# Moving the block placement of a triangular inverse from GpSimd to VectorE and ScalarE in a two-layer hybrid trunk

## The chip, the core and the metric

The kernel runs on one core of a Trainium2 chip. The metric is the device time of one execution in microseconds. The engines are named as in the profile: PE is TensorE, DVE VectorE, ACT ScalarE, POOL GpSimd, SP SyncE, which here issues DMAs. Each engine works through its own instructions strictly in order; semaphores tie the engines to each other.

## The reference

The kernel computes a trunk of two layers on 1024 frames of width 1024. Layer 0 mixes with two head groups side by side, eight RWKV-7 heads of 64 and four gated DeltaNet heads of 128. Layer 1 mixes with chunked attention of 16 heads. Each layer then has a squared-ReLU MLP of width 4096 and a gated per-layer embedding.

```python
for i in range(DEPTH):                                   # DEPTH = 2
    h = rmsnorm(x, norm_mix_g[i])
    if i % 2 == 0:
        y_a = rwkv7_group(...)                           # 8 heads x 64
        y_b = gdn_group(...)                             # 4 heads x 128
        mix = jnp.concatenate([y_a, y_b], -1) @ even_w_out[e]
    else:
        mix = chunk_band_attention(...) @ attn_w_out[o]
    x = x + mix
    hf = rmsnorm(x, norm_ffn_g[i])
    x = x + jnp.square(jax.nn.relu(hf @ mlp_w1[i])) @ mlp_w2[i]
    x = x + rmsnorm(p[i] @ ple_w_proj[i], ple_norm_g[i]) * jax.nn.sigmoid(x @ ple_w_gate[i])

# inside gdn_group, per chunk of 64 frames:
sol = lax.linalg.triangular_solve(amat, rhs, left_side=True, lower=True, unit_diagonal=True)
```

The triangular solve is what the change is about. The kernel solves it, for both head groups of layer 0, by inverting the unit triangular matrix of each chunk and head.

## The kernel before, in words

Layer 0's mixing takes the first 860 us or so; the MLP, the embedding and the whole of layer 1 follow. Layer 0's mixing is cut into 16 units, one behind the other: units 0 to 7 on the first 512 frames, 8 to 15 on the second, and in each half RWKV (a pair of heads) and DeltaNet (one head) in turn. Even units are RWKV and have eight 128 by 128 matrices to invert (two chunks of 64 side by side in each), odd units are DeltaNet and have four. A unit goes through the stages in, front, mid, back and post, each in a lane of its own. The lanes are Python generators that `Trunk.run` interleaves by estimated times; a scheduler then sets each engine's order by its own timeline of all instructions. Weights are split into a high and a low part (`whi` on ACT, L316, and `wlo` on DVE, L317), and products with them on TensorE (`dps`) fill the time between the lanes' small steps.

The inverse of a unit starts in its front. `inverse_start` (L405) writes the matrices N to DRAM (L409), reads their 16 by 16 diagonal blocks back as `subb` with one block to a partition (L413), and inverts all blocks at once on GpSimd by substitution (L421, L423, fourteen times L428 and L430, L431: result `sub`). It writes the result to DRAM as `z` (L433) and reads it as `Xp`, 128 partitions wide (L435). All these DMAs are on SP's queue.

`inverse_end` (L438), in the mid lane, then doubles the blocks: 16 to 32, 32 to 64, 64 to 128. Its steps, with `quad[i]` the partitions 32i to 32i+31:

- T16, Xp's transposes times a mask, on ACT (L455); TensorE's step 0 on them. GpSimd writes X2's left half, Xp times the mask (L461); ACT brings step 0 out as Z16 (L462).
- TensorE's step 1; DVE writes X2's right half (L468) and transposes X2, now the 32 by 32 inverses, into T2 (L469).
- TensorE's step 2 on T2; its results go to TZ, quad 1 by ACT and quad 3 by DVE (L480). GpSimd clears a corner of TZ (L481), copies T2's quads 0 and 1 into TZ (L483), and X2's four diagonal blocks into F, where the finished inverse is put together (L485).
- TensorE's step 3, copies to TZ (L492) and F (L494), and the last two steps with ACT's copies (L505).

TZ is taken anew from the pool `mid` for each inverse; Z16 and the two F tiles are permanent. TensorE's products of the inverse carry the name `iz`. Unit 14's neighbours in time are the weights and norms of the embedding (`xg`, `praw`, L1750 on). `PMQ` (L992) is an RWKV unit's masked product, which TensorE needs for `ch`; `S` is its state.

Of the kernel before, what the change touches and what calls it, by code (L numbers as in the profile page):

```python
# [8 lines left out]
F32 = mybir.dt.float32  # L9
# [3 lines left out]
ALU = mybir.AluOpType  # L13
# [4 lines left out]
P = 128  # L18
# [94 lines left out]
class Trunk:  # L113
# [324 lines left out]
    def inverse_end(self, Xp, B, N, F):  # L438

        nc, h2 = self.nc, self.mid  # L440
        V, A, G = nc.vector, nc.scalar, nc.gpsimd
        cur, curT = Xp[:, :, 0:16], Xp[:, :, 16:32]
        m1, m2 = self.half[:, 0:1], self.half[:, 1:2]
        quad = [slice(32 * i, 32 * i + 32) for i in range(4)]
# [5 lines left out]
        def new(nm, w):  # L450
            return h2.tile([P, N, w], F32, tag=nm, name=nm)
# [5 lines left out]
        for g in range(N):  # L457
            for q in quad:
                self.mm(pz[q, g, :], B[q, g, q], T1[q, g, :], start=True, stop=True)
        X2, T2 = new("X32", 32), new("T32", 32)  # L460
        G.tensor_scalar(X2[:, :, 0:16], cur, m1, None, op0=ALU.mult)  # L461
        A.activation(self.Z16[:, 0:N, 0:16], pz, AF.Copy, scale=m2)  # L462
# [5 lines left out]
        V.scalar_tensor_tensor(X2[:, :, 16:32], cur, m2, px, op0=ALU.mult, op1=ALU.add)  # L468
        V.transpose(T2.rearrange("p g c -> p (g c)"), X2.rearrange("p g c -> p (g c)"))  # L469
        yield f"inverse{N}_1"  # L470

        pz = bank(32)

        TZ = new("TZ", 64)
        Z = TZ[:, :, 0:32]
        for g in range(N):
            for i in (0, 2):
                self.mm(pz[quad[i + 1], g, :], B[quad[i], g, quad[i + 1]], T2[quad[i], g, :], start=True, stop=True)
        for i, cp in ((0, A.copy), (2, V.tensor_copy)):
            cp(Z[quad[i + 1]], pz[quad[i + 1]])  # L480
        G.memset(TZ[quad[0], :, 32:64], 0.0)  # L481
        for i in range(2):
            G.tensor_copy(TZ[quad[i], :, quad[i]], T2[quad[i]])  # L483
        for i in range(4):
            G.tensor_copy(F[quad[i], :, quad[i]], X2[quad[i]])  # L485
        yield f"inverse{N}_2"
# [29 lines left out]
    def layer0_in(self):  # L516
        nc, tc, a = self.nc, self.tc, self.a
        with ExitStack() as es:
# [3 lines left out]
            l0 = self.l0 = es.enter_context(self.pool("l0"))  # L522
# [24 lines left out]
            for t in self.F.values():  # L547
                for i in range(1, 4):
                    nc.gpsimd.memset(t[32 * i:32 * i + 32, :, 32 * (i // 2 * 2):32 * i] if i % 2 else t[64:128, :, 0:64], 0.0)

            self.bm = self.pre.tile([P, 2, 2, 2, C], F32, tag="ph", name="bm")
            for h in range(2):
# [306 lines left out]
    def rwkv_front(self, p, hf, sc, raws, u):  # L859
        nc, h2, fr, sm, psm = self.nc, self.h2, self.fr, self.sm, self.psm  # L860
        V, A, G = nc.vector, nc.scalar, nc.gpsimd
# [28 lines left out]
        L = fr.tile([P, 4, C + 1], F32, tag="LE", name="L", bufs=2)  # L890
        G.memset(L[:, :, 0:1], 0.0)
        for c in range(4):
# [1353 lines left out]
```

## Time and profile before

| what | value |
|---|---|
| median of 3 runs | 2970.08 us (2968.52 to 2975.79) |
| profiled execution | 2974.58 us |
| its span | 2972.9 us |
| mean granted TensorE clock | 0.986 |
| busy: PE, DVE, ACT, POOL | 97%, 71%, 49%, 15% of the span |
| PE busy from 100 to 860 us | 715.34 of 760 us |
| POOL busy from 100 to 860 us | 290.36 of 760 us |

A row of a group reads: line, engine, operation, output<-input, shapes, count | busy us, mean ns of one | idle time of the engine just before them, with what ended most of it. A row of the timeline reads: start, duration, engine, line, operation, count, and in brackets the idle time of the engine before it with what released it. A row of waits reads: who waited, for whom; us in total, times, longest.

### The profile page before, as it was taken

The numbers are of one execution on the slowest core, as the hardware profiler recorded it, in microseconds if no ns is written. First come the engines' busy times: TensorE is split into PE (matmuls) and PEld (weight loads), VectorE is DVE, ScalarE is ACT, GpSimd is POOL, SyncE is SP. The second block draws the span as 40 slices with busy tenths as digits, with TensorE's granted clock in tenths as the row PEclk, the third lists the DMA queues.
The fourth block names the chain that finished last, engine by engine and source line by source line (L and its number), as shares of the span: only waits on it lengthen the run. The fifth ranks groups of instructions, "written<-read, shape, count | busy, mean of one in ns | idle before, by whom it ended". The sixth has DMA issues, their size and how long they took to land.

```text
span 2972.9 us, 46975 instructions
## 1 busy us (share of the span) xinstructions
PE 2888.2 (97%) x17286; PEld 2418.2 (81%) x17286; DVE 2108.3 (71%) x4183; ACT 1463.3 (49%) x2892; POOL 442.4 (15%) x951
## 2 busy tenths in 40 slices
PE   8899999999999999999999999999999999999999
PEld 6677777777777888888888999999888888888887
DVE  7565664556749777787786677776868777877884
ACT  5353432334437555544444466665847455544441
POOL 5443432333500000000000111111300000000000
PEclk9998999999899999999999999999999999999999
DMA  6534323332447444754433211110376444754423
GB/s 222 193 126 149 110 67 133 121 107 92 138 153 237 159 149 142 263 171 151 156 110 128 80 49 44 59 56 21 118 244 202 149 149 156 268 169 151 147 95 117
DMA packets 205159, 412.52 MB, mean 139 GB/s; under 512 B 46352, under 2 KB 48640, under 8 KB 204928
## 3 DMA queue, kind: packets, MB, share of 16 engines
q1 hardware_dynamic: 174112, 353.40, 36.0%
q10 hardware_dynamic: 30816, 56.11, 4.9%
q8 instruction: 136, 2.23, 0.3%
q14 instruction: 95, 0.78, 0.1%
HBM read 283.54 MB, written 125.89 MB: 138 GB/s over the span
## 4 chain that ended last, share of the span: by engine, by line
PE 65%; DVE 6%; DMA 4%; ACT 2%; issue 1%; POOL 1%; SPq 0%; POOLq 0%; ACTq 0%; DVEq 0%
PE dps L180 58%; PE po L180 2%; PE pt L195 1%; DMA pn<-pnd 1%; PE sn L180 1%; PE ch L180 1%; DVE pb L2094 1%; PE sf L180 1%; DVE act L1326 0%; POOL sub L430 0%; PE iz L180 0%; DVE F L2036 0%; POOL subt L428 0%; PE dps L195 0%; DVE r L1326 0%
## 5 line engine op out<-in xcount | busy, mean ns | idle before, releaser
L180 PE MATMUL dps<-r,act 128*128 128x512 f32 x3720 | 873.7, 392 | 1.4 <-DVE r L1326 0.8
L180 PEld LDWEIGHTS dps<-r,act 128*128 128x128 f32 x3720 | 698.1, 188 | 156.2 <-DVE r L1326 1.2
L180 PE MATMUL dps<-xg,whi 128*128 128x512 f32 x1248 | 423.0, 419 | 17.3 <-ACT whi L316 12.0
L180 PE MATMUL dps<-wq,act 128*128 128x384 f32 x1536 | 302.8, 341 | 4.3 <-ACT act L365 1.8
L180 PEld LDWEIGHTS dps<-xg,whi 128*128 128x128 f32 x1248 | 230.6, 196 | 67.9 <-ACT whi L316 12.6
L180 PEld LDWEIGHTS dps<-wq,act 128*128 128x128 f32 x1536 | 263.8, 189 | 7.4 <-DVE vs L1977 2.3
L180 PE MATMUL dps<-xg,wlo 128*128 128x512 f32 x624 | 253.6, 407 | 1.2 <-DVE wlo L317 1.1
L1325 ACT CAST act<-act 128x512 fp32r<-128x512 f32 (+2 forms) x281 | 159.5, 600 | 150.0 <-PE dps L180 64.9
L1326 DVE TENSOR_TENSOR act<-act 128x512 fp32r<-128x512 f32 (+2 forms) x281 | 178.1, 662 | 5.6 <-ACT act L1325 5.6
L180 PE MATMUL dps<-act 128*128 128x512 f32 x720 | 174.7, 391 | 0.9 <-DVE late L1447 0.9
L1325 ACT CAST act<-late 128x512 fp32r<-128x512 f32 x210 | 123.7, 620 | 104.4 <-PE dps L180 81.8
L180 PE MATMUL dps<-late,act 128*128 128x512 f32 x672 | 166.5, 392 | 0.0
L1326 DVE TENSOR_TENSOR act<-late,act 128x512 fp32r<-128x512 f32 x210 | 139.3, 687 | 33.3 <-ACT act L1325 33.2
L180 PEld LDWEIGHTS dps<-act 128*128 128x128 f32 x720 | 135.1, 188 | 30.8 <-DVE late L1447 1.4
L180 PEld LDWEIGHTS dps<-late,act 128*128 128x128 f32 x672 | 126.0, 188 | 27.7
L180 PEld LDWEIGHTS dps<-xg,wlo 128*128 128x128 f32 x624 | 121.9, 195 | 30.3 <-DVE wlo L317 3.4
L180 PE MATMUL dps<-xw,act 128*128 128x512 f32 x576 | 145.7, 392 | 0.4 <-DVE act L1326 0.4
L1593 DVE TENSOR_TENSOR xw<-xw,dps 128x512 f32<-128x512 f32 x192 | 130.1, 682 | 15.9 <-PE dps L180 15.8
L180 PEld LDWEIGHTS dps<-xw,act 128*128 128x128 f32 x576 | 107.9, 188 | 25.0 <-DVE act L1326 0.9
L1847 POOL MEMSET far<- 128x256 f32 x1 | 0.3, 316 | 799.7 <-PE dps L180 799.7
L2100 ACT ACTIVATE pb<-pb,mx 128x640 f32<-128x640 f32 (+4 forms) x128 | 89.2, 697 | 52.5 <-DVE mx L2094 51.5
L1325 ACT CAST r<-act 128x512 fp32r<-128x512 f32 x126 | 76.2, 617 | 57.0 <-PE dps L180 33.2
(517 smaller groups left out, 5363.2 us busy)
## 6 DMA issues: line engine op xcount, KB each, us to landing
hb<-late ACTq DMA_DIRECT2D x196, 256.0 KB
act<-hb SPq DMA_DIRECT2D x158, 256.0 KB
late<-in_w SPq DMA_DIRECT2D x60, 512.0 KB
act<-in_w SPq DMA_DIRECT2D x112, 256.0 KB
braw<-hb SPq DMA_DIRECT2D x80, 256.0 KB
wd<-whi SPq DMA_DIRECT2D x28, 512.0 KB
wd<-wlo SPq DMA_DIRECT2D x28, 512.0 KB
whi<-wd SPq DMA_DIRECT2D x28, 512.0 KB
```

What stands on the lines that cost most here:

```text
L180: return self.begin(self.nc.tensor.matmul(out, lhsT, rhs, start=start, stop=stop, skip_group_check=again))
L195: return self.begin(self.nc.tensor.transpose(out, in_, ident))
L1325: A.copy(hi, s)
L1326: V.tensor_tensor(lo, s, hi.bitcast(F32), op=ALU.subtract)
L1593: V.tensor_tensor(x[n][:, hs[hf]], x[n][:, hs[hf]], ps, op=ALU.add)
L1847: nc.gpsimd.memset(self.far, 0.0)
L2094: V.tensor_tensor_reduce(pb[:, (j0 - f0) * P:(j0 - f0 + n) * P], ps[:, 0:n * P], t, op0=ALU.add, op1=ALU.min, scale=-1.0, scalar=mx[:, 0:1 ...
L2100: A.activation(S, S, AF.Exp, bias=mx[:, 1:2] if nf else mx[:, 0:1], scale=-1.0, accum_out=l)
```

## The change

The change rewrites who does the small moves in `inverse_end`:

- TZ becomes one permanent tile, whose corner is cleared once when layer 0 is set up. T2 is no tile of its own any more: it is TZ's left columns.
- DVE's one transpose of 128 partitions becomes two that write into TZ: partitions 0 to 95 into the left columns (also step 2's operand), and quad 1 into the columns 32 to 63. GpSimd's two copies (L483) and its memset (L481) go.
- X2's left half is written by DVE instead of GpSimd (L461 before, L462 after).
- F's four diagonal blocks are copied by DVE (quads 2 and 0) and ACT (3 and 1) instead of GpSimd (L485 before, L482 after).
- The first column of the scan tile L in the RWKV front is cleared by DVE instead of GpSimd (L891 before, L890 after).

Lines from L461 to L480 stand one further down in the new file or keep their number; those behind some way up to about L890 stand three to one further up (L492 becomes L489, L505 becomes L502, L992 becomes L991).

```diff
--- before.py
+++ after.py
@@ -438,7 +438,7 @@
     def inverse_end(self, Xp, B, N, F):
 
         nc, h2 = self.nc, self.mid
-        V, A, G = nc.vector, nc.scalar, nc.gpsimd
+        V, A = nc.vector, nc.scalar
         cur, curT = Xp[:, :, 0:16], Xp[:, :, 16:32]
         m1, m2 = self.half[:, 0:1], self.half[:, 1:2]
         quad = [slice(32 * i, 32 * i + 32) for i in range(4)]
@@ -457,8 +457,9 @@
         for g in range(N):
             for q in quad:
                 self.mm(pz[q, g, :], B[q, g, q], T1[q, g, :], start=True, stop=True)
-        X2, T2 = new("X32", 32), new("T32", 32)
-        G.tensor_scalar(X2[:, :, 0:16], cur, m1, None, op0=ALU.mult)
+        X2, TZ = new("X32", 32), self.TZ[:, 0:N]
+        T2, Z = TZ[0:96, :, 0:32], TZ[:, :, 0:32]
+        V.tensor_scalar(X2[:, :, 0:16], cur, m1, None, op0=ALU.mult)
         A.activation(self.Z16[:, 0:N, 0:16], pz, AF.Copy, scale=m2)
         yield f"inverse{N}_0"
         px = bank(16)
@@ -466,23 +467,19 @@
             for q in quad:
                 self.mm(px[q, g, :], self.Z16[q, g, :], cur[q, g, :], start=True, stop=True)
         V.scalar_tensor_tensor(X2[:, :, 16:32], cur, m2, px, op0=ALU.mult, op1=ALU.add)
-        V.transpose(T2.rearrange("p g c -> p (g c)"), X2.rearrange("p g c -> p (g c)"))
+        V.transpose(T2, X2[0:96])
+        V.transpose(TZ[quad[1], :, 32:64], X2[quad[1]])
         yield f"inverse{N}_1"
 
         pz = bank(32)
 
-        TZ = new("TZ", 64)
-        Z = TZ[:, :, 0:32]
         for g in range(N):
             for i in (0, 2):
                 self.mm(pz[quad[i + 1], g, :], B[quad[i], g, quad[i + 1]], T2[quad[i], g, :], start=True, stop=True)
         for i, cp in ((0, A.copy), (2, V.tensor_copy)):
             cp(Z[quad[i + 1]], pz[quad[i + 1]])
-        G.memset(TZ[quad[0], :, 32:64], 0.0)
-        for i in range(2):
-            G.tensor_copy(TZ[quad[i], :, quad[i]], T2[quad[i]])
-        for i in range(4):
-            G.tensor_copy(F[quad[i], :, quad[i]], X2[quad[i]])
+        for i, cp in ((2, V.tensor_copy), (3, A.copy), (0, V.tensor_copy), (1, A.copy)):
+            cp(F[quad[i], :, quad[i]], X2[quad[i]])
         yield f"inverse{N}_2"
         px = bank(32)
         for g in range(N):
@@ -548,6 +545,8 @@
                 for i in range(1, 4):
                     nc.gpsimd.memset(t[32 * i:32 * i + 32, :, 32 * (i // 2 * 2):32 * i] if i % 2 else t[64:128, :, 0:64], 0.0)
 
+            self.TZ = l0.tile([P, 8, 64], F32, tag="TZ", name="TZ")
+            nc.gpsimd.memset(self.TZ[0:32, :, 32:64], 0.0)
             self.bm = self.pre.tile([P, 2, 2, 2, C], F32, tag="ph", name="bm")
             for h in range(2):
                 nc.gpsimd.memset(self.bm[64 * (1 - h):64 * (2 - h), :, h], 0.0)
@@ -888,7 +887,7 @@
         A.activation(lw, psw, AF.Tanh, bias=self.dv["hw0"][:, p:p + 1], scale=0.5)
         V.tensor_scalar(lw, lw, -0.5 * EXPM05, -0.5 * EXPM05, op0=ALU.mult, op1=ALU.add)
         L = fr.tile([P, 4, C + 1], F32, tag="LE", name="L", bufs=2)
-        G.memset(L[:, :, 0:1], 0.0)
+        V.memset(L[:, :, 0:1], 0.0)
         for c in range(4):
             V.tensor_tensor_scan(L[:, c, 1:C + 1], self.ones, lw[:, c * C:(c + 1) * C], 0.0,
                                  op0=ALU.mult, op1=ALU.add)
```

TensorE issues the same number of instructions; DVE issues 72 more, ACT 32 more, POOL 135 fewer. The table of estimated times is the same in both kernels; the scheduler orders anew. From the end of layer 0's mixing on the order of every engine is the same as before. In the part that changes, SP gets the small transfers z, Xp and subb of some units ahead of weight loads that stood before them, and ACT in unit 0's inverse has T16 of the next unit and then the cast `bh` ahead of the TZ copy, where before it had `bh`, T16 and the TZ copy.

Unit 2 on DVE, before, from the product f of a later unit on to the second PMQ:

```order
L1122 SCALAR_TENSOR_TENSOR f<-f 128x512
L1146 TENSOR_TENSOR cs<-cs,gs_beta 128x4
L868 SCALAR_TENSOR_TENSOR f<-raw,vecs,f 128x512
L1050 SCALAR_TENSOR_TENSOR S_1987<-S_1923,ee,ch 128x64
L1147 TENSOR_SCALAR ncs<-cs 128x4
L992 TENSOR_TENSOR PMQ<-pm,mask_136 128x384
L1014 SCALAR_TENSOR_TENSOR Sh<-S_1987,ee,blkr 128x128
L1014 SCALAR_TENSOR_TENSOR Sh<-Sr_184,ee,blkr 128x128
L992 TENSOR_TENSOR PMQ<-pm,mask_136 128x384
```

And after, from the same f on:

```order
L1121 SCALAR_TENSOR_TENSOR f<-f 128x512
L1144 TENSOR_TENSOR cs<-nu 128x4
L1147 SCALAR_TENSOR_TENSOR hin<-ss,nu 128x4
L867 SCALAR_TENSOR_TENSOR f<-raw,vecs,f 128x512
L462 TENSOR_SCALAR X_2505<-Xp,half 128x8x16
L1145 TENSOR_TENSOR cs<-cs,gs_beta 128x4
L1049 SCALAR_TENSOR_TENSOR S_1985<-S_1921,ee,ch 128x64
L991 TENSOR_TENSOR PMQ<-pm,mask_136 128x384
L1146 TENSOR_SCALAR ncs<-cs 128x4
L1013 SCALAR_TENSOR_TENSOR Sh<-S_1985,ee,blkr 128x128
L1013 SCALAR_TENSOR_TENSOR Sh<-Sr_184,ee,blkr 128x128
L991 TENSOR_TENSOR PMQ<-pm,mask_136 128x384
```

X2 of unit 2 (`X_2505`) is new here, and S, PMQ and Sh, which stood behind the last f, now stand behind X2.

Unit 14 on DVE, before, in the norm of an earlier unit (vv, rv, rsw) and the split of an embedding weight (wlo):

```order
L707 TENSOR_TENSOR gate<-dps,acc 128x512
L1204 SCALAR_TENSOR_TENSOR W<-ch,gs_egc,b 128x128
L1073 TENSOR_SCALAR vv<-pp 128x8
L294 TENSOR_SCALAR rv<-vv 128x8
L297 TENSOR_TENSOR rsw<-rv 128x8
L298 SCALAR_TENSOR_TENSOR rsw<-rsw,vv 128x8
L299 SCALAR_TENSOR_TENSOR rv<-rsw,rv 128x8
L317 TENSOR_TENSOR wlo<-wraw,whi 128x1024
```

And after:

```order
L706 TENSOR_TENSOR gate<-dps,acc 128x512
L1203 SCALAR_TENSOR_TENSOR W<-ch,gs_egc,b 128x128
L1072 TENSOR_SCALAR vv<-pp 128x8
L294 TENSOR_SCALAR rv<-vv 128x8
L297 TENSOR_TENSOR rsw<-rv 128x8
L462 TENSOR_SCALAR X_9046<-Xp,half 128x8x16
L298 SCALAR_TENSOR_TENSOR rsw<-rsw,vv 128x8
L317 TENSOR_TENSOR wlo<-wraw,whi 128x1024
L299 SCALAR_TENSOR_TENSOR rv<-rsw,rv 128x8
```

X2 of unit 14 (`X_9046`) has come between L297 and L298, ahead of wlo.

Unit 4's substitution on POOL, before:

```order
L421 AFFINE_SELECT sub<-subb 64x16x16
L423 AFFINE_SELECT sub<-sub 64x16x16
L705 COPY raw<-h_g_192 128x3
L428 TENSOR_TENSOR subt<-sub,subb 64x14
L430 TENSOR_TENSOR sub<-sub,subt 64x14
L428 TENSOR_TENSOR subt<-sub,subb 64x2x13
L485 COPY F_230<-X_3087 32x4x32 x2
L430 TENSOR_TENSOR sub<-sub,subt 64x2x13
L485 COPY F_230<-X_3087 32x4x32 x2
L483 COPY TZ<-T_3088 32x4x32 x2
```

And after:

```order
L421 AFFINE_SELECT sub<-subb 64x16x16
L423 AFFINE_SELECT sub<-sub 64x16x16
L428 TENSOR_TENSOR subt<-sub,subb 64x14
L430 TENSOR_TENSOR sub<-sub,subt 64x14
L428 TENSOR_TENSOR subt<-sub,subb 64x2x13
L430 TENSOR_TENSOR sub<-sub,subt 64x2x13
```

The copies of unit 3 into F (`F_230`) and TZ have gone from between the first steps of the substitution, and a copy into `raw` has moved further back.

## The prediction

> **What bounds the kernel now.** I read the busy time in three windows first, to see which stage the change can reach; then the chain that ended last; then what TensorE waited for in the first 900 us; then the timeline round each of its inverse waits. The order of instructions on every engine is the same in both kernels from about 860 us on (the end of layer 0's mixing), so only the first two windows count. Columns: width, then busy time of PE, PE weight loads, DVE, ACT and POOL, the granted clock, DMA share, GB/s.
>
> ```profile
> 0.00:100.00 100.00, 89.61 (x404) 69.09 (x405) 69.52 (x129) 48.91 (x85) 54.69 (x133) 0.98 0.67 239
> 100.00:860.00 760.00, 715.34 (x6615) 572.46 (x6614) 456.60 (x1108) 298.43 (x730) 290.36 (x721) 0.95 0.36 119
> 860.00:2972.90 2112.90, 2083.20 (x10272) 1776.65 (x10270) 1582.22 (x2947) 1116.00 (x2078) 97.39 (x98) 1.00 0.42 141
> ...
> PE 65%; DVE 6%; DMA 4%; ACT 2%; issue 1%; POOL 1%; SPq 0%; POOLq 0%; ACTq 0%; DVEq 0%
> ```
>
> TensorE is the bound throughout. In the window of the 16 inverses (100 to 860 us) it is busy 715.34 of 760 us: 44.7 us of idle time, plus what the clock of 0.95 takes, is all that any rearrangement of small copies can win there. GpSimd, with 290.36 us, is far from full, and so are DVE and ACT. The next view gives how much of the idle time is the inverse's own (columns: total, times, longest).
>
> ```profile
> PE iz L180 <- DVE TZ L480: 10.2, 2, 9.3
> PE iz L180 <- ACT T L455: 6.6, 4, 2.5
> POOL sub L421 <- DMA subb<-scr: 83.8, 14, 23.1
> POOL X L461 <- DMA Xp<-z: 64.4, 14, 7.5
> ```
>
> TensorE lost 10.2 + 6.6 us in inverses. In 14 of 16 units the substitution begins by waiting for the DMA that brings its blocks (83.8 us), so GpSimd being free earlier does not start them sooner. And the X2 multiply, which the change hands to VectorE, waited 64.4 us for the DMA of Xp: on GpSimd that wait hurt nobody, on VectorE it may.
>
> **What leaves GpSimd.** These groups go (busy, mean ns, idle before):
>
> ```profile
> L485 POOL COPY F<-X 32x256 f32<-32x256 f32 x32 | 14.3, 447 | 23.7 <-DVE X L468 18.1 <-DVE rsw L302 4.3
> L485 POOL COPY F<-X 32x128 f32<-32x128 f32 x32 | 13.9, 434 | 28.2 <-DVE X L468 27.1
> L483 POOL COPY TZ<-T 32x128 f32<-32x128 f32 x16 | 7.3, 459 | 1.7 <-DVE T L469 0.8 <-DVE cc L914 0.2
> L483 POOL COPY TZ<-T 32x256 f32<-32x256 f32 x16 | 7.2, 451 | 0.7
> L461 POOL TENSOR_SCALAR X<-Xp,half 128x128 f32<-128x128 f32 x8 | 5.8, 729 | 37.3 <-DMA Xp<-z 37.3
> L461 POOL TENSOR_SCALAR X<-Xp,half 128x64 f32<-128x64 f32 x8 | 3.7, 465 | 32.2 <-DMA Xp<-z 27.1 <-PE iz L180 3.2 <-PE ch L180 2.0
> ```
>
> 14.3 + 13.9 + 7.3 + 7.2 + 5.8 + 3.7 = 52.2 us of busy time, and the small memsets. It is worth something only where a copy stood inside a later unit's substitution, because Xp then comes that much earlier.
>
> **What VectorE and ScalarE get.** Nearest rows of the same shapes:
>
> ```profile
> L469 DVE STREAM_TRANSPOSE T<-X 128x256 f32<-128x256 f32 x8 | 3.5, 438 | 0.2
> L469 DVE STREAM_TRANSPOSE T<-X 128x128 f32<-128x128 f32 x8 | 2.4, 300 | 0.1
> L480 DVE COPY TZ<-iz 32x256 f32<-32x256 f32 x8 | 3.4, 429 | 11.9 <-ACT TZ L480 11.7
> L468 DVE SCALAR_TENSOR_TENSOR X<-Xp,half,iz 128x128 f32<-128x128 f32 x8 | 2.7, 343 | 1.9 <-PE iz L180 0.9 <-issue 0.7 <-POOL sub L430 0.3
> L480 ACT COPY TZ<-iz x16: 257/310/364, 144.7 to 838.9; 32x256 f32<-32x256 f32 x8, 32x128 f32<-32x128 f32 x8
> ```
>
> VectorE per inverse: X2 at most 0.34 us, one transpose more (0.44 or 0.30), two F copies at most 0.43 each, so 1.64 us in a unit of eight matrices and 1.50 in one of four, 8 x 3.14 = 25 us at most in all. ScalarE: 2 x 0.31 x 16 = 10 us. Against 456.60 and 298.43 us busy in 760 us neither becomes the bound; what covers these is idle time of the two engines. The cover is thin where TensorE waits right behind the second transpose or an F copy; the F copies stand behind the TZ copies, which TensorE needs first. The bounds are 0 and 16 x 0.44 = 7 us (every added transpose on the path); I take +2, nearer to nothing since TensorE works on other lanes meanwhile and waits in few inverses at all.
>
> **Unit 4, where GpSimd's copies did hurt.**
>
> ```profile
> 261.81 1.54 POOL L485 COPY F<-X 32x128 f32<-32x128 f32 x2 [0.19 <-DVE X L468]
> 263.72 0.98 POOL L485 COPY F<-X 32x128 f32<-32x128 f32 x2
> 264.76 1.11 POOL L483 COPY TZ<-T 32x128 f32<-32x128 f32 x2
> ...
> 271.14 0.45 PE L180 MATMUL iz<-TZ,Ng 64*64 64x64 f32 x8 [1.51 <-POOL sub L430]
> ...
> 285.43 0.72 PE L180 MATMUL iz<-T,N 32*32 32x16 f32 x64 [1.71 <-ACT T L455]
> 286.98 1.65 PE L180 MATMUL pm<-AR,bm 128*128 128x128 f32 x4 [0.82 <-ACT tm L1004]
> ```
>
> Six copies of unit 3 (1.54 + 0.98 + 1.11 = 3.6 us) stand inside unit 4's substitution, and the stall at 271.14 is TensorE's wait for GpSimd at the same place. Without them T of unit 4 is there 3.6 us earlier, more than 1.71 + 0.82. All three stalls go: 1.51 + 1.71 + 0.82 = -4.0 us. Bounds: 0 (the transfers are late anyway) to -4.0; I take -4.0, since the rows name these releasers.
>
> **Unit 5.**
>
> ```profile
> 308.01 0.18 POOL L709 COPY h_r<-raw 128x1 f32<-128x1 f32 x1 [3.46 <-DVE raw L707]
> ...
> 327.50 0.35 ACT L455 ACTIVATE T<-Xp,half 128x64 f32<-128x64 f32 x1 [7.77 <-DMA Xp<-z]
> 328.88 1.05 PE L180 MATMUL pp<-ones,o 128*128 128x1 f32 x8 [2.03 <-ACT o L1222]
> ```
>
> This substitution was held 3.46 us by a halo copy; now that copy stands behind it. Xp then lands near 324 instead of 327.50, and the 2.03 us stall, an ACT result queued behind T, goes. X2 on VectorE now holds a cast, L707 and a weight split behind it, estimated at +0.8. Net -1.2; bounds -2.0 and +2.7 (Xp not earlier: the split about as late as X2 is).
>
> **Unit 1: the largest stall stays.**
>
> ```profile
> 145.69 0.26 PE L180 MATMUL iz<-X,TZ 32*32 32x32 f32 x2 [9.28 <-DVE TZ L480]
> ...
> 140.00:160.00 20.00, 14.31 (x128) 11.59 (x129) 4.89 (x8) 8.24 (x21) 4.17 (x13) 0.75 0.34 114
> ```
>
> DVE's TZ copy names itself here, but it was itself behind ScalarE's TZ copy, which is queued behind T of the next unit, which waits for Xp. In the new order T still stands ahead, with the bh cast now between: +0.8 (one 512-wide cast; between 0 and that). The granted clock of 0.75 in this stretch shows what a long stall costs besides itself. [...]
>
> **Unit 2: the new wait on VectorE.**
>
> ```profile
> 172.85 1.86 POOL L485 COPY F<-X 32x128 f32<-32x128 f32 x4
> 175.03 0.63 POOL L483 COPY TZ<-T 32x128 f32<-32x128 f32 x2
> ...
> 181.73 0.55 DVE L992 TENSOR_TENSOR PMQ<-pm,mask 128x384 f32<-128x384 f32 x1
> ...
> 183.15 0.55 PE L180 MATMUL ch<-b,PMQ 128*128 128x64 f32 x4
> 187.01 0.40 ACT L455 ACTIVATE T<-Xp,half 128x128 f32<-128x128 f32 x1 [3.50 <-DMA Xp<-z]
> ```
>
> In the new order X2 of unit 2 stands ahead of S and PMQ, which released TensorE's ch at 183.15. Xp comes 1.86 + 0.63 = 2.5 us earlier, near 184.5. Then X2 0.34, two small ones and PMQ 0.55 bring ch to about 185.6: +2.4 us. If Xp is not earlier, +4.9. I take +2.4, because both copy rows lie inside the substitution.
>
> **Unit 14: the same, and worse.**
>
> ```profile
> 740.88 0.17 DVE L297 TENSOR_TENSOR rsw<-rv 128x8 f32<-128x8 f32 x1
> 756.24 0.40 ACT L455 ACTIVATE T<-Xp,half 128x128 f32<-128x128 f32 x1 [4.65 <-DMA Xp<-z]
> 756.70 0.36 PE L180 MATMUL iz<-T,N 32*32 32x16 f32 x20 [2.47 <-ACT T L455]
> ```
>
> X2 now stands right behind the L297 of 740.88, with the rest of the norm and two weight splits behind it; in the old run Xp was used at 756.24, 15.4 us later. In the new order the blocks' DMAs go ahead of two activation loads and the front of this unit is issued some 6 us earlier (an estimate from the TensorE work that it is moved ahead of), and X2 leads Xp's arrival by less, but I expect VectorE to stand still for about 6 us of it and TensorE to lose 6.5 us in place of the 2.47: +4. Bounds 0 (the front comes early enough) and +11 (15.4 less the work that TensorE has queued, about 2, and the 2.47 that goes).
>
> The other units' X2 cost at most some tenths each, +0.5 in all; queue SP gets the inverse's small transfers earlier and weight loads a little later, which I cost at nothing, since the casts that use them come many us later; without that cover a late weight load would show as a TensorE wait for a whi or wlo.
>
> **Sum.** +2 (added transposes) - 4.0 (unit 4) - 1.2 (unit 5) + 0.8 (unit 1) + 2.4 (unit 2) + 4 (unit 14) + 0.5 = +4.5 us. The profiled execution took 2974.58 us (span 2972.9 and 1.7 around it), 4.5 above the median of 2970.08; 2974.58 + 4.5 = 2979.1 for a like execution, 2974.6 for the median. 0.3%, 8.9 us, is about what a measurement of this kernel can tell from no change, so the likeliest is no change, at 2974.
>
> **The rivals.** *Slower:* VectorE's in-order wait for Xp. It decides if Xp is not earlier than before: then unit 2 costs 4.9, unit 5 +2.7, unit 14 +11, with +2, +0.8 and +0.5 as above and no gain at unit 4: 22 us, 2992. For it speaks the 64.4 us that X2 waited on GpSimd; against it that the substitutions lose 2.5 to 3.6 us of copies in just the units where it matters. Chance 0.26. *Faster, by shorter substitutions:* unit 4's and 5's stalls go (4.0 + 2.0), the rest of T's waits too (6.6 - 1.71 = 4.9), and the 9.28 by a third as T's Xp comes earlier; X2 costs nothing: 6.0 + 4.9 + 3 = -14, 2956. The 83.8 us of waits for blocks speak against it. Chance 0.19. *Faster, by less contention:*
>
> ```profile
> L919 DVE TENSOR_TENSOR f<-f 128x512 f32<-128x512 f32 x7 | 6.5, 928 | 0.0
> L1326 DVE TENSOR_TENSOR act<-act 128x512 fp32r<-128x512 f32 (+2 forms) x281 | 178.1, 662 | 5.6 <-ACT act L1325 5.6
> ```
>
> The same elementwise operation takes 928 ns on VectorE while GpSimd works and 662 where it rests. With 52.2 of 345 us of GpSimd gone a sixth of this goes: (928 - 662) / 6 = 44 ns on each of about 500 (nearly half of the 1108 that VectorE runs in the window), 22 us of VectorE, of which half on the path would be -11: 2959. [...] Most of VectorE's time is off the path, so chance 0.07. *Nothing is felt:* all copies were hidden before and are now, 2970; it lies inside the likeliest case, which has 0.48 in all.
>
> **How the numbers follow.** Same 0.48; slower 0.26; faster 0.19 + 0.07 = 0.26. The range reaches from 2956 to 2990: beyond lie some 2 in 10, the far ends of the faster and the slower cases.
>
> **What would show it.** Right: no T copy of GpSimd and no stall at units 4's places; stalls of 2 to 6 us on TensorE released by PMQ near 184 and by a weight split or a norm near 745; the 9 us stall near 145 unchanged; DVE 25 us busier or less. Wrong: VectorE's X2 waits for Xp for under 2 us in all units (then the sum is near -6), or TensorE's idle time after X2 in units that I cost at tenths.

## The result: 2989.7 us, slower by 0.77%

The changed kernel takes 2989.70 us in the median of 6 runs (2986.82 to 2998.80), the kernel before beside it 2969.68 (2958.49 to 2975.79): a ratio of 1.0077, 95% interval 1.0053 to 1.0101. The forecast was no change, at 2974. The executions of one kernel lie up to 17 us apart before and 12 after; the profiled one of the changed kernel, 2998.17 us with a span of 2996.5, is one of its slowest. That 2989.70 lies just inside the end of the forecast range, 2990, is luck: the sum did not lead there. Two slow executions further down, 3624.87 us with the weight loads first (granted clock 0.747) and 6140.41 us with X2 alone (1.0), are left out of the times given there.

The same three windows, after (columns as in the prediction):

```profile
0.00:100.00 100.00, 87.79 (x382) 67.37 (x383) 66.59 (x125) 46.81 (x81) 47.95 (x119) 0.95 0.64 222
100.00:860.00 760.00, 705.46 (x6498) 565.01 (x6497) 462.47 (x1169) 307.74 (x753) 239.68 (x600) 0.94 0.35 118
860.00:2996.50 2136.50, 2102.39 (x10411) 1790.19 (x10408) 1593.75 (x2963) 1122.14 (x2091) 96.80 (x98) 1.00 0.42 141
```

In the second window GpSimd is 51 us less busy, but TensorE too does less: 705 for 715 us. In the first 880 us, before and after:

```profile
0.00:880.00 880.00, 823.08 (x7096) 655.84 (x7097) 535.88 (x1257) 354.73 (x826) 345.06 (x853) 0.95 0.40 134
```

```profile
0.00:880.00 880.00, 811.49 (x7010) 646.14 (x7011) 537.80 (x1308) 360.20 (x846) 287.63 (x718) 0.95 0.38 130
```

TensorE stands idle for 68.5 us where it stood for 56.9. The granted clock, summed up finer than the two digits of these rows, takes another 47.8 us where it took 40.7. So of the 24 us between these two executions about 12 are idle time and about 7 clock in this part.

The time that GpSimd got back became waiting. Who waited, in the first 900 us, after:

```profile
POOL sub L421 <- DMA subb<-scr: 146.6, 14, 22.9
ACT T L455 <- DMA Xp<-z: 74.3, 14, 14.7
DVE X L462 <- DMA Xp<-z: 42.3, 15, 7.5
PE iz L180 <- DVE TZ L480: 8.6, 4, 5.9
```

GpSimd waits 146.6 us for the blocks where it waited 83.8, and VectorE has a new wait of 42.3 us for Xp.

To see where TensorE lost time, its matmuls, which are the same in all the kernels, are counted as work at their usual spacing; what a stretch took beyond its work is lost in it. The sizes are estimates, since they depend on the spacing that is taken as usual; the differences between the columns move by 1 to 2 us with it. From one profiled execution each (us lost):

| stretch of TensorE's work (us) | before | changed | old work, new order | moved work, old order | new order, X2 late |
|---|---|---|---|---|---|
| 0 to 20 (to about 35 us) | 11.3 | 15.9 | 11.3 | 15.8 | 15.7 |
| 20 to 100 | 12.3 | 14.3 | 12.1 | 14.2 | 14.0 |
| 100 to 160 | 30.7 | 36.9 | 37.4 | 34.8 | 34.7 |
| 160 to 260 (units 3 to 5) | 41.2 | 37.8 | 42.1 | 30.8 | 36.1 |
| 260 to 340 | 33.3 | 37.7 | 43.4 | 36.8 | 36.3 |
| 340 to 520 | 43.1 | 44.5 | 40.6 | 47.1 | 40.4 |
| 520 to 700 (to the end of the mixing) | 51.5 | 57.0 | 56.6 | 49.4 | 60.3 |
| the rest of the kernel | 55.5 | 58.2 | 57.3 | 51.2 | 52.4 |

(The last three columns are experiments, below.) The changed kernel loses more at the start, round unit 2, in the stretch behind unit 5 (260 to 340) and in the one that holds unit 14, and 3.4 us less round units 3 to 5. The last row moves by 4 to 6 us between kernels with the same order there (51.2 and 55.5 in the old order, 52.4 to 58.2 in the new), so a single row of one execution is worth no more than that. The column of the moved work in the old order shows that kernel's fastest execution, 2975.86 us against a median of 2984.71: what the moved work costs is not in it.

Two corrections of what stands ahead: a DeltaNet or RWKV unit has four chunks of 128 frames (the eight matrices are four chunks of two heads), and the order differs at one more place, a few rows at the end of layer 1's attention, where the trace shows no loss that the other kernels with that order share.

### The profile page after: what moved, and what is told of

Same layout as the page of the kernel before. It is cut to its first block, busy times and chain, and to the rows that moved or that the text cites. A ratio compares the mean times of both kernels' runs of the same rounds, so it can differ in the third digit from the quotient of the medians.

```text
span 2996.5 us, 46894 instructions
## 1 busy us (share of the span) xinstructions
PE 2895.6 (97%) x17286; PEld 2422.6 (81%) x17286; DVE 2122.8 (71%) x4255; ACT 1476.7 (49%) x2924; POOL 384.4 (13%) x816
## 4 chain that ended last, share of the span: by engine, by line
PE 67%; DVE 13%; DMA 9%; ACT 3%; POOL 3%; issue 3%; SPq 0%; ACTq 0%; DVEq 0%; POOLq 0%
PE dps L180 56%; PE po L180 2%; DVE act L1325 2%; PE ch L180 2%; POOL subt L428 1%; PE pt L195 1%; POOL sub L430 1%; PE iz L180 1%; PE sn L180 1%; PE pm L180 1%; DMA late<-in_w 1%; DMA pn<-pnd 1%; DMA Xp<-z 1%; PE tp L180 1%; DMA wraw<-in_w_out 1%
## 5 line engine op out<-in xcount | busy, mean ns | idle before, releaser
L180 PE MATMUL po<-ptile,vs 128*128 128x256 f32 (+1 forms) x576 | 98.6, 282 | 5.3 <-ACT ptile L362 2.7
```

The lines of the kernel that those rows point to most:

```text
L180: return self.begin(self.nc.tensor.matmul(out, lhsT, rhs, start=start, stop=stop, skip_group_check=again))
```

## The experiments

**How an order is held.** In the kernels called "order tied" the list of an engine's instructions is taken from another kernel, one list for each engine, and each instruction is made to issue behind its forerunner, by an edge for order alone as the kernel itself sets them at L189 and L326. The tie added no time that a run shows: with the old order tied and X2 alone moved the ratio is 0.9996 (0.9985 to 1.0008). The lists themselves are left out here.

So work and order can be changed apart. Each ratio below is against the kernel before run beside the experiment, whose median lay between 2968.9 and 2972.0 us; compare ratios rather than times. Theory A was VectorE's wait for Xp (the prediction's slower rival), B the newly drawn order, C the added busy time.

### Work and order apart

Moved work, old order:

> The changed kernel's instructions, but every engine's order tied to that of the kernel before, so that the order is not drawn anew; X2's left half stands right ahead of the X2 multiply-add that follows it on VectorE (so it never waits for Xp there), the two transposes where the one was, the F copies right behind them, on ScalarE ahead of its TZ copy. Theory A (what costs is VectorE standing still for Xp in X2): about 2970, as before. Theory B (what costs is the order drawn anew, weight loads behind z among it): about 2970. Theory C (the added busy time of VectorE and ScalarE costs): 2980 or more. If GpSimd's relief gives something back, 2960 to 2966.

Measured: 2984.71 us, ratio 1.0045 (1.0030 to 1.0059). Of the three theories only C foresaw this.

Old work, new order:

> The kernel before's instructions, with the order of all instructions that both kernels have tied to that of the changed kernel, on every engine; the ones that only the kernel before has (GpSimd's copies, memsets and X2, VectorE's one transpose) are placed freely by the scheduler. VectorE never waits for Xp in X2, and GpSimd does the small moves. Theory A: 2970 to 2974. Theory B: 2985 to 2992. Theory C: about 2970.

Measured: 2992.06 us, 1.0075 (1.0060 to 1.0090). So this order costs the old work as much as the whole change costs, though in it VectorE never waits for Xp in X2; and the moved work costs 14 us in the old order, in which nothing was redrawn. Theories A and B alone fail on the first of these, theory C alone on the second. The two costs don't add up to more than 1.0077, and why is not shown. One rival for part of the second is untested: GpSimd's copies, memset and X2 are in no held list there, and where the scheduler put them some stand ahead of a later unit's substitution, which costs by itself (see the run up to unit 5 below).

The new order, with X2 alone moved in VectorE's list:

```diff
 # VectorE's list of the changed kernel, for each of the 16 units
-[..., X2 (L462), 6 to 56 rows of other work, X's other half (L469), ...]
+[..., 6 to 56 rows of other work, X2 (L462), X's other half (L469), ...]
```

> The changed kernel with its own order on every engine, in which one thing is moved: X2's left half on VectorE stands right ahead of the multiply-add that writes X2's other half, 6 to 56 rows later, where Xp has long landed. VectorE's 42 us of waits for Xp go. Theory A: 2972 to 2976, 14 to 18 us less than the changed kernel. Theory B: 2984 to 2990; only the stall at unit 2 (3.5 us and its half clock) goes, since the stall at unit 14 is released by a weight load. Theory C: 2988.

Measured: 2986.77 us, 1.0060 (1.0047 to 1.0074), against 1.0077 (1.0053 to 1.0101) for the changed kernel: 0.17% less by the ratios, 5 us (3 us by the medians), for 42 us of VectorE's waits, and the intervals overlap. Why so little can be seen at unit 2. TensorE's stall there in the changed kernel, then in this one, then with the old work in the new order:

```profile
193.03 1.11 PE L180 MATMUL ch<-b,PMQ 128*128 128x64 f32 x4 [3.47 <-DVE S L1049]
```

```profile
193.46 0.45 PE L180 MATMUL iz<-F,TZ 64*64 64x64 f32 x8 [2.25 <-ACT TZ L502]
```

```profile
189.05 0.48 PE L180 MATMUL iz<-F,TZ 64*64 64x64 f32 x4 [3.90 <-ACT TZ L505]
```

X2's wait is gone in the second and was never there in the third, and TensorE stands still all the same, for a step of an inverse. That this step now comes too early in TensorE's list is likely from these rows, but no run moved it alone.

Unit 14, with SP's list alone changed:

```diff
 # SP's list of the changed kernel at unit 14
-z<-sub, wraw<-in_w_ple, Xp<-z, wraw<-in_w_ple
+wraw<-in_w_ple, wraw<-in_w_ple, z<-sub, Xp<-z
```

> The changed kernel with its own order on every engine, in which one thing is moved: on SP's queue the two loads of the embedding's weight stand ahead of unit 14's z again, as they did before, and no longer behind its wait for GpSimd. Theory A: no change but tenths, 2989, since VectorE still waits 6.6 us for Xp there and the next weight split stands behind it. Theory B: the stall of 4.9 us for the weight goes, 2983 to 2985.

Measured: 2990.84 us (five executions), 1.0066 (1.0050 to 1.0082): no gain on the changed kernel's 1.0077 that the intervals would show. The changed kernel at that place, SP's queue, VectorE, ScalarE and TensorE:

```profile
757.02 0.45 SPq L433 DMA_DIRECT2D z<-sub  x1
757.57 0.53 SPq L310 DMA_DIRECT2D wraw<-in_w_ple  x1
...
764.21 0.28 DVE L462 TENSOR_SCALAR X<-Xp,half 128x128 f32<-128x128 f32 x1 [6.65 <-DMA Xp<-z]
...
761.64 1.04 ACT L316 CAST whi<-wraw 128x1024 fp32r<-128x1024 f32 x1 [7.36 <-DMA wraw<-in_w_ple]
...
762.74 2.07 PE L180 MATMUL dps<-xg,whi 128*128 128x512 f32 x4 [4.92 <-ACT whi L316]
```

VectorE waits 6.65 us for Xp, as forecast. But what holds TensorE for 4.92 us is a weight: its load stands behind z in SP's list, z waits for GpSimd's substitution to end (757.02), and the load is issued at 757.57. With the loads ahead of z:

```profile
762.51 1.19 PE L180 MATMUL dps<-xg,whi 128*128 128x512 f32 x4 [0.74 <-ACT whi L316]
766.75 0.71 PE L180 MATMUL iz<-T,N 32*32 32x16 f32 x34 [3.05 <-ACT T L455]
```

The stall is 0.74, and a new one of 3.05 us stands 4 us later, for the Xp that now comes second.

### One engine's order

TensorE's list alone tied to the old one, and TensorE's list alone tied to the new one:

> The changed kernel with only TensorE's order tied to that of the kernel before; the scheduler orders the other engines as it likes. Theory B, in the form that TensorE's newly drawn order does it (steps of the inverse with less other work between them): 2970 to 2976, most of the 20 us gone. Theory B in the form that the order of the other engines does it, or theory A (VectorE's waits for Xp): 2983 to 2990.

> The kernel before with only TensorE's order tied to that of the changed kernel; the scheduler orders the other engines as it likes. TensorE's order does it: 2985 to 2992. The other engines' orders do it: 2968 to 2975.

Measured: 2998.87 us, 1.0092 (1.0079 to 1.0105), and 2986.00 us, 1.0049 (1.0037 to 1.0061). The first lies outside all that was expected: the old list of TensorE did not bring the time back (1.0092 against 1.0077, intervals overlapping). The second is what was expected if TensorE's order does it. Neither run changes TensorE's list by itself, because the scheduler draws the other lists to fit: in the second, 91 of some 1250 VectorE operations in the first 900 us stand out of the order of "old work, new order", 202 out of the old one. In the first VectorE's list comes nearer to that of "moved work, old order" than to the changed kernel's (124 against 235 out of place), and yet the time is the worst of all, where exactly the old order gave 1.0045. So a list near the old one is not enough, and which engine's list costs most stays open.

The old work tied to the new order only up to unit 5 (330 us), and to the old one behind:

> The kernel before's instructions, tied to the changed kernel's order up to unit 5's inverse (about 330 us) and to the old order from there on. The profile of the kernel with the new order throughout had lost 7 to 9 us by that place of its 20: 2977 to 2980. If the new order does harm only as a whole: 2970 or 2990.

Measured: 2993.24 us, 1.0076 (1.0063 to 1.0088): as much as the new order throughout, where 7 to 9 us were expected. That does not show that the first third is enough. In its profile about 6 us are lost up to unit 5's place, near what was expected. Another 12 us are lost in one stretch where the old order holds again (450 to 490 us of the kernel before), where no other kernel's profile loses more than 4. GpSimd and TensorE there:

```profile
460.80 0.30 POOL L481 MEMSET TZ<- 32x256 f32 x1 [11.44 <-PE iz L180]
462.05 0.50 POOL L421 TENSOR_SCALAR_AFFINE_SELECT sub<-subb 64x256 f32<-64x256 f32 x1 [0.95 <-DMA subb<-scr]
...
474.88 1.11 PE L195 MATMUL pp<-ident,o 128*128 128x128 f32 x4 [3.55 <-DVE o L1076]
...
487.25 0.37 PE L180 MATMUL iz<-T,N 32*32 32x16 f32 x18 [3.37 <-ACT T L455]
```

The memset of TZ, which no list holds, stands ahead of the unit's substitution and waits 11.44 us for TensorE. Before, the same substitution began at 452.98, with the memset inside it. So this run measures its own seam as much as the order.

X2 on ScalarE behind T16, everything drawn anew:

```diff
-        V.tensor_scalar(X2[:, :, 0:16], cur, m1, None, op0=ALU.mult)
+        A.activation(X2[:, :, 0:16], cur, AF.Copy, scale=m1)
```

> The changed kernel with X2's left half written by ScalarE, right behind T16, which waits for the same Xp there anyway; nothing is tied, the scheduler orders all engines anew. Theory A: the waits of VectorE are gone, 2972 to 2976. Theory B: any order can come out; if the new one is as bad as the changed kernel's, 2985 to 2990. Theory C (added busy time): as the changed kernel, 2988.

Measured: 2983.16 us (2976.30 to 2994.38), 1.0046 (1.0030 to 1.0062): between the times that the theories named, and level with the moved work in the old order. Without any wait for Xp on VectorE the change still costs.

### One part of the change alone

With the old order tied (short diffs against the kernel before):

```diff
 # F copies alone
-        for i in range(4):
-            G.tensor_copy(F[quad[i], :, quad[i]], X2[quad[i]])
+        for i, cp in ((2, V.tensor_copy), (3, A.copy), (0, V.tensor_copy), (1, A.copy)):
+            cp(F[quad[i], :, quad[i]], X2[quad[i]])
 # X2 alone
-        G.tensor_scalar(X2[:, :, 0:16], cur, m1, None, op0=ALU.mult)
+        V.tensor_scalar(X2[:, :, 0:16], cur, m1, None, op0=ALU.mult)
 # transposes alone: the permanent TZ and the lines of the change on it and T2, nothing else
```

> The kernel before with its own order tied, and one part of the change alone: F's four diagonal blocks are copied by VectorE (quads 2 and 0, right behind the transpose) and ScalarE (3 and 1, right ahead of its TZ copy). If the first experiment's 14 us come from VectorE's added busy time in the inverses, this part (two of VectorE's four added instructions, some 0.45 us per inverse) gives about 4 to 6 of it, against a gain of 4 at unit 4, whose substitution no longer holds copies: 2969 to 2974. If only the start costs, 2966 to 2968.

> The kernel before with its own order tied, and one part alone: X2's left half on VectorE, right ahead of the multiply-add behind it, where Xp has landed (0.25 to 0.29 us per inverse on VectorE, between TensorE's steps 1 and 2). Added busy time: 2972 to 2975. Else 2970.

> The kernel before with its own order tied, and one part alone: the permanent TZ, cleared once on GpSimd at the start, and the two transposes in place of one and GpSimd's copies into TZ. The start costs 4.5 us if GpSimd's shifted setup decides that (VectorE's xg operations 2.0 to 2.5 us); the second transpose 0.2 to 0.4 us per inverse: 2974 to 2978. Without the start's loss 2970 to 2973.

The same three parts as the change writes them, the order drawn anew:

> The F copies alone on VectorE and ScalarE (the part of the change that cost 5 us with the old order), now written as the change writes it, with nothing tied: the scheduler draws the order anew. If drawing anew costs as such, since the order of the kernel before is an unusually good one: 2980 to 2990. If the new order of the changed kernel was bad luck: anything from 2965 to 2985, and the three kernels of this kind differ in sign.

> X2's left half alone on VectorE, with nothing tied. With the old order and X2 late this part cost nothing. Here the scheduler also puts X2 ahead of work that does not wait for Xp. Drawing anew costs as such, or VectorE's waits for Xp do: 2980 to 2990. Luck: 2965 to 2985.

> The permanent TZ and the two transposes alone, with nothing tied. With the old order this part cost 8 us, about 4 of them at the start. Drawing anew costs as such: 2985 to 2995. Luck: 2970 to 2990.

| part alone | old order tied | order drawn anew |
|---|---|---|
| F copies | 2974.93, 1.0018 (1.0007 to 1.0029) | 2976.62, 1.0024 (1.0013 to 1.0034) |
| X2 | 2968.86, 0.9996 (0.9985 to 1.0008) | 2969.28, 0.9996 (0.9987 to 1.0005) |
| transposes and TZ | 2978.24, 1.0030 (1.0019 to 1.0041) | 2981.95, 1.0038 (1.0026 to 1.0051) |
| sum of the three | +0.44% | +0.58% |
| all together | 1.0045 (the first experiment) | 1.0077 (the changed kernel) |

In the old order the parts add up to the whole (0.44 and 0.45%; the memset of L, moved too, was not run alone). X2 costs nothing in either column; drawn anew its VectorE waits for Xp are there too:

```profile
DVE X L461 <- DMA Xp<-z: 31.0, 12, 7.1
```

So 31 us of waiting on VectorE cost nothing in sum in that order. A draw of the scheduler doesn't cost as such: three of them took 0 to 4 us more than their tied twins, with intervals that overlap.

F copies all on ScalarE, old order tied (`A.copy` for all four):

> The kernel before with its own order tied; F's four blocks are all copied by ScalarE, right ahead of its TZ copy, and VectorE gets nothing. If VectorE's added time is what costs and GpSimd's copies inside the substitutions did hurt: 2964 to 2968, faster than before. If ScalarE's four copies (1.1 us) ahead of TZ are on the path: 2973 to 2980.

Measured: 2977.72 us (2966.38 to 2989.24), 1.0027 (1.0013 to 1.0041): VectorE is not the only engine on which the copies cost. The expectation for ScalarE's copies being on the path was met.

### The start

TZ's clearing in the setup has no term in the prediction's sum. VectorE at the start, before, and in the changed kernel:

```profile
13.12 2.74 DVE L366 SCALAR_TENSOR_TENSOR xg<-f,vecs,xg 128x512 fp32r<-128x512 f32 x2 [0.38 <-ACT xg L365]
15.78 1.21 DVE L317 TENSOR_TENSOR wlo<-wraw,whi 128x1024 fp32r<-128x1024 f32 x1
```

```profile
12.95 4.44 DVE L366 SCALAR_TENSOR_TENSOR xg<-f,vecs,xg 128x512 fp32r<-128x512 f32 x2 [0.38 <-ACT xg L365]
17.31 2.29 DVE L317 TENSOR_TENSOR wlo<-wraw,whi 128x1024 fp32r<-128x1024 f32 x1
```

And GpSimd beside them, before and changed:

```profile
13.57 1.74 POOL L694 TENSOR_TENSOR acc<-acc,f 128x512 f32<-128x512 f32 x1
```

```profile
13.62 1.26 POOL L693 TENSOR_TENSOR acc<-acc,f 128x512 f32<-128x512 f32 x1
```

The same operations run beside each other, and who is slowed is swapped: before, GpSimd (1.74 us for 1.26), after, VectorE (4.44 for 2.74, 2.29 for 1.21). TensorE waits for that xg, before and changed:

```profile
14.22 0.50 PE L180 MATMUL dps<-xg,whi 128*128 128x512 f32 x1 [0.44 <-DVE xg L366]
15.92 0.49 PE L180 MATMUL dps<-xg,whi 128*128 128x512 f32 x1 [0.73 <-DVE xg L366]
```

```profile
15.49 0.50 PE L180 MATMUL dps<-xg,whi 128*128 128x512 f32 x1 [1.91 <-DVE xg L366]
17.44 0.80 PE L180 MATMUL dps<-xg,whi 128*128 128x512 f32 x1 [0.99 <-DVE xg L366]
```

and its granted clock is lower, 0.89 for 1.00; from 10 to 40 us, before and changed:

```profile
10.00:40.00 30.00, 28.20 (x127) 20.07 (x127) 19.29 (x29) 13.45 (x23) 24.58 (x30) 1.00 0.63 234
```

```profile
10.00:40.00 30.00, 26.95 (x107) 19.18 (x106) 16.50 (x24) 12.81 (x22) 19.89 (x26) 0.89 0.58 214
```

Three kernels test whether GpSimd's setup, longer by one memset, decides it:

```diff
 # first experiment, and the changed kernel: TZ cleared on VectorE
-            nc.gpsimd.memset(self.TZ[0:32, :, 32:64], 0.0)
+            nc.vector.memset(self.TZ[0:32, :, 32:64], 0.0)
 # kernel before, order tied: one superfluous memset there
+            nc.gpsimd.memset(self.F[8][32:64, :, 0:32], 0.0)
```

> The first experiment (moved work, old order), with the one memset that clears TZ's corner at the start moved from GpSimd to VectorE, so that GpSimd's setup is 0.3 us shorter again. In the first 40 us the changed kernel and the first experiment both lost 4.5 us against the kernel before, after VectorE's operations for xg took 2.0 to 2.5 us in place of 1.0 to 1.6 beside GpSimd's squares. If GpSimd's shifted setup decides that: no such loss, 4 to 5 us less than the first experiment, and VectorE's xg operations near 1 us. If it is chance or something else: the same as the first experiment.

> The kernel before with its own order tied, and one superfluous GpSimd memset of 32 partitions by 256 (0.3 us) more in the setup, between the memsets of F and of bm, where the changed kernel clears TZ. Nothing else differs. If GpSimd's shifted setup costs at the start: VectorE's xg operations at 13 to 17 us take 2.0 to 2.5 us, TensorE's work of the first 40 us ends 4 to 5 us later, and the time is 2973 to 2975. If what is lost at the start comes back later in waits for the substitutions: 2970 to 2972. If the start's loss has another cause: 2970, and no longer xg operations.

> The changed kernel as it is, with the one memset that clears TZ's corner on VectorE in place of GpSimd, so that GpSimd's setup is as long as before. If the start's loss counts: 2984 to 2986, 4 to 5 us less than the changed kernel. If it comes back later: 2989 to 2990.

Measured: the first experiment with TZ cleared on VectorE 2985.79 us, 1.0050 (1.0038 to 1.0062): the start's loss is gone from its profile, not from the time. The kernel before with one memset more 2975.26 us, 1.0020 (1.0009 to 1.0030). The changed kernel with TZ cleared on VectorE 2985.61 us, 1.0054 (1.0039 to 1.0068). VectorE in the last two:

```profile
13.22 4.73 DVE L366 SCALAR_TENSOR_TENSOR xg<-f,vecs,xg 128x512 fp32r<-128x512 f32 x2 [0.38 <-ACT xg L365]
```

```profile
13.20 0.75 DVE L366 SCALAR_TENSOR_TENSOR xg<-f,vecs,xg 128x512 fp32r<-128x512 f32 x1 [0.39 <-ACT xg L365]
14.33 1.73 DVE L366 SCALAR_TENSOR_TENSOR xg<-f,vecs,xg 128x512 fp32r<-128x512 f32 x1 [0.39 <-ACT xg L365]
```

A memset of 0.3 us in GpSimd's setup makes the kernel before slower by 0.20%, 6 us, and taking it out of the changed kernel moves it from 1.0077 to 1.0054. The first number is clear of noise; the intervals of the other two overlap. In the first experiment the gain did not arrive. Its profile, of the median execution, shows where it went: the 4.4 us won at the start are lost again at 95 to 125 us, ahead of the first move of an inverse that changed hands (136 us). Windows and TensorE's stall there, in the kernel before, in the changed kernel with TZ cleared on VectorE, and in the first experiment with it:

```profile
110.00:130.00 20.00, 17.95 (x214) 14.09 (x213) 16.13 (x41) 11.04 (x21) 7.99 (x13) 1.00 0.77 272
113.72 0.70 PE L180 MATMUL dps<-xg,whi 128*128 128x512 f32 x2 [1.79 <-ACT f L877]
```

```profile
110.00:130.00 20.00, 17.26 (x200) 13.39 (x200) 15.86 (x44) 10.63 (x20) 7.95 (x17) 0.91 0.73 263
113.16 0.70 PE L180 MATMUL dps<-xg,whi 128*128 128x512 f32 x2 [2.49 <-ACT f L876]
```

```profile
110.00:130.00 20.00, 17.22 (x111) 12.47 (x110) 10.20 (x29) 6.37 (x10) 7.19 (x19) 0.66 0.67 233
114.53 0.70 PE L180 MATMUL dps<-xg,whi 128*128 128x512 f32 x2 [2.53 <-ACT f L876]
```

The stall is the same as in the second kernel, but the clock is 0.66 for 0.91 over 20 us, 5 us of work. Whether it is so in every execution of that kernel is not shown.

### Where the new order loses

The changed kernel with TZ cleared on VectorE has the changed kernel's order on every engine, but for that memset. So there are five profiles with the new order and two with the moved work in the old one. Below are the us that each took beyond the kernel before for the same TensorE work (estimates, with each matmul's work taken as the median spacing of its shape; the stretches are times of the kernel before):

| stretch | changed | TZ on VectorE | X2 late | weights first | old work, new order | moved work, old order | the same, TZ on VectorE |
|---|---|---|---|---|---|---|---|
| 7 to 40 (start) | 4.8 | 0.1 | 4.4 | 4.9 | 0.0 | 4.4 | 0.0 |
| 95 to 125 | 1.9 | 2.2 | 1.8 | 1.7 | -0.3 | 1.9 | 6.6 |
| 155 to 195 (unit 2) | 6.4 | 6.1 | 4.2 | 6.5 | 6.8 | 0.9 | 0.9 |
| 365 to 400 | 5.6 | 5.9 | 4.0 | 7.4 | 10.3 | 1.9 | 2.2 |
| 730 to 830 (unit 14 and behind) | 6.3 | 6.2 | 8.7 | 5.7 | 6.3 | 0.2 | 1.5 |
| all else | -1.4 | -9.7 | -12.1 | -2.7 | -1.0 | -8.1 | 0.0 |

At three places every kernel with the new order loses 4 to 10 us, and neither with the old order more than 2.2. The prediction had terms for the first and the last, and none for 365 to 400 us. There TensorE's waits are short in the changed kernel (none over 1.5 us), but the granted clock is 0.73, for 0.93 in the same part before. Changed, and before:

```profile
373.00:398.00 25.00, 22.33 (x239) 17.83 (x243) 18.20 (x70) 11.82 (x39) 8.56 (x22) 0.73 0.13 33
```

```profile
365.00:390.00 25.00, 24.26 (x270) 19.64 (x270) 21.44 (x85) 12.58 (x41) 12.59 (x35) 0.93 0.20 55
```

What the redraw costs in all is less sure, since both orders also win and lose elsewhere. With TZ cleared on GpSimd the moved work takes 1.0045 in the old order and 1.0077 in the new one; with TZ cleared on VectorE, 1.0050 and 1.0054. That is 9 us by one pair and 1 us by the other, and in neither are the intervals apart.

No version was faster than the kernel before: X2 alone is level with it, and all else is slower.

## Why the prediction was wrong

- **The direction.** No change at 2974 was forecast; it is slower by 20 us. The slower rival named 2992, near what came, but for a reason that the runs don't bear out: VectorE's wait for Xp. It waited as forecast (6.65 us at unit 14, 4.7 at unit 2), yet X2 alone costs nothing in two kernels, and taking all its waits out of the new order wins 3 to 5 us of 20, within the noise.
- **Added work, "+2 (added transposes)", mis-sized: the step that failed most.** The moved work by itself, in the old order and with X2 where it waits for nothing, takes 13 to 15 us more (1.0045, and 1.0050 with TZ cleared on VectorE). Measured by parts, the F copies take +0.18%, 5 us, and the transposes with TZ +0.30%, 9 us. The bound of 7 us was taken from the transposes alone; the F copies, which "stand behind the TZ copies" in the prediction, stand ahead of them on both engines in every inverse of the new order, so the reason to price them at nothing did not hold. Through which waits these microseconds come is not shown: one execution differs from the next by as much, and the granted clock goes with it only in part (in the first experiment, 2975.86 us at a mean clock of 0.987 and 2990.09 at 0.983, but also 2982.46 at 0.987). Of the two profiles with the old order one is the fastest execution, and the other lost most where no inverse's move had begun.
- **TZ's clearing at the start, no term at all.** One memset of that size costs the kernel before 0.20% (0.09 to 0.30), with VectorE's two xg operations at 4.73 us for 2.74. In the changed kernel the difference points the same way, and in the moved work with the old order it does not show.
- **The order, looked at in six places.** The prediction priced the places where the order tables showed a wait and took the rest as it was. A third place, at 365 to 400 us, loses as much as each of the two that it named, and the old work takes 0.75% more in the new order. The change of the whole order had no term in the sum and no rival. What it adds to the moved work lies between 1 and 9 us by the two pairs above.
- **Unit 4, -4.0: right there, given back near by.** No stall of TensorE is released by GpSimd's substitution or T any more at those places, and the stretch round units 3 to 5 loses 3.4 us less (10 less in the fastest execution of the old order), though one execution can move a stretch by that much. New stalls stand close to it, and take a part back:

```profile
286.09 0.66 PE L195 MATMUL pm<-ident,bk 128*128 128x128 f32 x4 [2.09 <-DVE PMQ L991]
...
323.75 0.49 PE L180 MATMUL ch<-Sg,KQ 128*128 128x128 f32 x2 [3.35 <-DVE Sg L1214]
```

- **Unit 5, -1.2: not separable.** Its 2.03 us stall behind T is gone. The 3.35 us stall above, behind Sg on VectorE, stands next to that place and is none that the prediction names.
- **Unit 2, +2.4 (to 4.9): right mechanism, not its worth.** The 3.47 us stall behind S is there; without X2's wait 2.25 us return under another name, and the place still loses 4.2 of 6.4 us.
- **Unit 14, +4: about the size, wrong releaser.** The stall is 4.92 us in place of the 2.47 before (6.5 was forecast), but for the weight behind z in SP's list, which the prediction put "at nothing, since the casts that use them come many us later". It had named the sign of that error, a wait for whi.
- **Unit 1, +0.8 with the 9.28 us kept: wrong.** The stall shrank, why is not shown:

```profile
151.70 0.26 PE L180 MATMUL iz<-X,TZ 32*32 32x32 f32 x2 [5.93 <-DVE TZ L480]
```

- **Less contention (faster, 2959): refuted as a gain.** The first row that it rested on holds one long operation: over all eight of that line before, the median is 682 ns and the longest 2387. The 662 ns beside it are of another operation, on `act`, with other shapes mixed in; its 128x512 form takes 686. The mean of the first row did fall, from 928 to 683 ns,

```profile
L918 DVE TENSOR_TENSOR f<-f 128x512 f32<-128x512 f32 x7 | 4.8, 683 | 0.0
```

but that is 1.7 us over 7 operations. The 1091 operations of VectorE that both kernels run, and that the kernel before starts between 100 and 860 us, sum up to 501.7 us before and 496.4 after: 5 us, where the rival had 22. At the start, where operations of the two stand beside each other, the times go together (GpSimd 1.74 us with VectorE 2.74, or 1.26 with 4.44), and there the change cost time instead of winning it.
- **The clock.** The prediction's sum holds no clock; it names one only at the 9.28 us stall (0.75 over 20 us). In the runs a lower clock also stands beside shorter waits: at the start waits of 1.9 and 1.0 us, against 0.4 and 0.7, come with a granted clock of 0.89 for 1.00 over 30 us, which is 3.3 us of work, near 114 us a wait of 2.5 us comes with 0.91 or 0.66 over 20 us, and behind the 3.47 us stall of unit 2 in the changed kernel it is 0.50 from 192 to 198 us.

## What to carry to other kernels

A change that lets a scheduler draw anew is two changes: hold the order of the old kernel and measure the moved work by itself, then let the order go. Work that leaves an idle engine for a busier one is not free because its sum fits into idle time, and idle time won on an engine that waits for a transfer can go into a longer wait (146.6 us for 83.8 here). A long wait in a trace is worth what its removal brings: 31 and 42 us of VectorE's waits were worth 0 and 3 to 5 us. An experiment that holds an order has to hold every instruction: one memset left free waited 11.44 us in front of a substitution. And a profile is one execution: a loss counts as the order's when it comes back at the same place in every kernel with that order.

## What the runs showed of the hardware that was not expected

At the start GpSimd's 128x512 add and VectorE's two xg operations stand beside each other, and their times come in pairs: GpSimd 1.73 to 1.75 us with VectorE 2.69 to 2.74, or 1.26 to 1.29 with 4.44 to 4.73. The first pair came in ten of the eleven profiles without the further memset of 0.3 us on GpSimd, the second in all nine with it. The eleventh shows a third way: in the changed kernel with TZ cleared on VectorE, 0.75 and 1.73 us on VectorE stand beside 1.28 on GpSimd.

The granted clock was not the same beside like stalls. With 2.49 us of waiting near 113 us, in the changed kernel with TZ cleared on VectorE, it was 0.91 over 20 us, 1.8 us of work; with 2.53 us near 114, in the first experiment with it, 0.66, 6.8 us; with 1.79 us in the kernel before it was 1.00.
